# RWKV-7 inverse in a decoder step: three transfers of 68 and 34 rows, each split into two pieces

## The chip, the cores and the metric

The kernel runs on one core of a Trainium2 chip. The time is that of one execution on the device, in microseconds (us), from the launch of the program to its end; the median of three runs stands for a kernel. A profile is one further execution, recorded by the hardware profiler; its span runs from the first to the last instruction.

## The reference

One layer of a hybrid decoder is computed for 1024 prompt tokens and 8 samples of 8 tokens (1088 columns in all), with four token mixers side by side (HGRN2, RWKV-7, a convolution module, RG-LRU), then gates, output projection and an MLP. What matters here is the RWKV-7 mixer, which is a recurrence over tokens in each of 8 heads of width 64:

```
def step(s, inp):
    rt, wt, kt, vt, kkt, at = inp
    sa = jnp.einsum("bhvk,bhk->bhv", s, -kkt)
    s = s * wt[:, :, None, :] + sa[..., None] * (kkt * at)[:, :, None, :] + vt[..., None] * kt[:, :, None, :]
    return s, jnp.einsum("bhvk,bhk->bhv", s, rt)
```

All inputs and outputs are float32.

## The kernel before, in words

All matrices of the layer are multiplied on TensorE (PE) in blocks of 128 x 128, each product as three (high part by high part, low by high, high by low), into PSUM tiles named pg. The weights of a block are loaded by SP into wst, and ScalarE (ACT) and VectorE (DVE) form the high and low parts whi and wlo from them. The mixers run in four rounds (the string ROUNDS sets their order); each round has one RWKV block of two heads, one HGRN2 head pair, one convolution part and one RG-LRU part, and gate products fill PE in between. The generators of the mixers are written one after the other, and a scheduler with a cost model decides in which order the instructions stand on each engine. On an engine they then run strictly in that order.

An RWKV block (rw_block) does not walk through the tokens one by one. It takes chunks of 64 tokens, 16 of the prompt and one with the samples, so that with two heads there are 34 triangular systems of 64 x 64 to solve. For this, the unit triangular matrices are inverted. Each is cut into two diagonal blocks of 32 x 32 and one block beside them. The steps:

- PE computes the products G, DVE masks them into the tiles Gt (lines 554 to 565), and SP writes the diagonal blocks to DRAM, to za (line 569). za has the shape 2 x 34 x 32 x 32: half, unit, row, column.
- SP reads za back with one 32 x 32 block in each partition: 2 x 34 = 68 rows of 4 KB, tile At (line 585). Partition is now the unit, so that DVE can work on all 68 blocks at once.
- In 31 steps of two instructions each (lines 589 to 594), DVE forms the inverses in Zu.
- DVE copies the first 34 of them transposed into the place of At (line 596), SP writes Zu to DRAM as zb (68 rows of 4 KB, line 598) and the transposed copy as zx (34 rows of 4 KB, line 599).
- SP reads zx back into the tile X1 (line 602: 32 partitions with 34 pieces of 128 bytes each) and zb into the G tiles (lines 606 and 607: ten reads).
- PE multiplies: zq from X1 and the block beside the diagonal, ACT copies it into X1, zz from that copy and zb, ACT copies it into G (lines 608 to 620). Then the recurrence over the 17 chunks begins (line 631 on).

In between, the weights' reads stand in the same queue of SP: what is queued behind a read of zb that waits for its write stands still with it. The reads of zb stand for the writes of zb, that of X1 for the write of zx. The first matmuls that need X1 are zq; PE's queue holds pg products before and behind them. In PE's order the adaptive-norm weights (tile adaw, matmuls ada) come some 45 us behind zq in each round.

Of the kernel before, what the change touches and what calls it, by code (L numbers as in the profile page):

```python
# [90 lines left out]
class Net:  # L91
# [382 lines left out]
    def rw_block(self, j):  # L474
        nc = self.nc
# [22 lines left out]
        a, sg, wd = self.flat("a", 4), self.flat("sg", 5), self.flat("wd", 2)  # L498
# [52 lines left out]
        za = self.dp.tile([2, 34, 32, 32], F32, name="za", tag="za", bufs=2)  # L551
        zb = self.dp.tile([2, 34, 32, 32], F32, name="zb", tag="zb", bufs=2)
        zx = self.dp.tile([34, 32, 32], F32, name="zx", tag="zx", bufs=2)
# [28 lines left out]
        At = At_t[0:68, 0:1024].rearrange("p (i t) -> p i t", t=32)  # L582
        Zu_t = self.flat("Zu", 5)
        Zu = Zu_t[0:68, 0:1024].rearrange("p (i t) -> p i t", t=32)
        nc.sync.dma_start(At, za.rearrange("a u i t -> (a u) i t"))
        nc.gpsimd.memset(Zu_t[0:68, 0:1024], 0.0)
        nc.gpsimd.memset(Zu_t[0:68, 0:1024:33], 1.0)
        tm_t = self.rp.tile([128, 512], F32, name="tm", tag="vk", bufs=2)
        for i in range(31):
            r, m = i + 1, 31 - i  # L590
# [4 lines left out]
        xt_t = At_t  # L595
        nc.vector.tensor_copy(xt_t[0:34, 0:1024].rearrange("p (t i) -> p t i", i=32),
                              Zu[0:34].rearrange("p i t -> p t i"))
        nc.sync.dma_start(zb.rearrange("a u i t -> (a u) i t"), Zu)
        nc.sync.dma_start(zx, xt_t[0:34, 0:1024].rearrange("p (t i) -> p t i", i=32))

        X1 = self.flat("X1", 1)[:, 0:1088].rearrange("p (u t) -> p u t", t=32)
        nc.sync.dma_start(X1[64:96], zx.rearrange("u i t -> i u t"))
# [949 lines left out]
```

## Time and profile before

| | us |
|---|---|
| median of 3 runs | 2525.07 |
| lowest and highest | 2517.87, 2526.18 |
| profiled execution | 2528.64 |
| its span | 2526.9 |
| PE busy | 2430.2 (96%) |
| DVE busy | 1381.1 (55%) |
| ACT busy | 1037.1 (41%) |
| POOL busy | 330.2 (13%) |

The mean granted clock of TensorE over the span is 0.981 of full speed. The DMA engines move 300.46 MB in 185111 packets, 119 GB/s in the mean.

To read it: a row of a timeline has the start and the duration in us, the engine, the line, the operation, the written tile, an arrow and the read tiles, the shapes, the count, and in brackets the idle time of the engine before it with what ended it. The engine SPq is SP's queue of DMA issues; the duration of such a row is the issue, not the transfer. Buffer numbers are left out: X is X1, and At in a row of line 596 is the transposed copy. L98, L101, L104 and L107 are the lines of the helpers for ACT, DVE and PE, so that the tile says which instruction it is. In a list of waits stand the total in us, the number of times and the longest. In a table by stretches, a busy time is followed by the number of instructions in brackets; the granted clock (1.00 is full speed), the mean busy share of the 16 DMA engines and the GB/s end the row.

### The profile page before, as it was taken

What the parts mean: (1) busy time and instruction counts of PE and PEld (TensorE: products, weight loads), DVE (VectorE), ACT (ScalarE), POOL (GpSimd) and SP (SyncE); (2) the same over time, 40 slices, a digit from 0 to 9 for tenths busy, and PEclk for the clock granted to TensorE, in tenths of its full rate; (3) what the DMA queues carried; (4) which work ended last, traced back from release to release, by engine and by line L of the source; (5) the groups of instructions that cost most, each with busy time, mean ns of one, the idle gap of its engine ahead of it and who ended that gap; (6) DMA issues with size and microseconds to landing.
All of it is one profiled execution on the core that took longest, in us unless ns stands there. A gap on an engine that the chain in (4) does not pass through costs nothing.

```text
span 2526.9 us, 46611 instructions
## 1 busy us (share of the span) xinstructions
PE 2430.2 (96%) x19086; PEld 2255.0 (89%) x19086; DVE 1381.1 (55%) x2536; ACT 1037.1 (41%) x1855; POOL 330.2 (13%) x503
## 2 busy tenths in 40 slices
PE   6999999999999999999999999998899999999996
PEld 2897899898888988989888899998899999999996
DVE  6664626637365555457553667668755552422247
ACT  4512434323454235442244653346666665111115
POOL 3101210103100021101012000000222221000003
PEclk9999999999999999999999999999999999999998
DMA  6323132223221232112313455533565557434144
GB/s 242 120 85 91 56 104 68 70 74 98 92 68 63 81 97 97 68 62 80 98 60 105 163 186 169 194 114 104 157 157 157 157 153 257 137 139 184 61 158 132
DMA packets 185111, 300.46 MB, mean 119 GB/s; under 512 B 57385, under 2 KB 97273, under 8 KB 184897
## 3 DMA queue, kind: packets, MB, share of 16 engines
q1 hardware_dynamic: 134480, 217.79, 27.1%
q0 software_dynamic: 47104, 74.44, 9.7%
q10 hardware_dynamic: 3312, 5.25, 0.6%
q8 instruction: 150, 2.46, 0.4%
q14 instruction: 65, 0.52, 0.1%
HBM read 211.29 MB, written 81.66 MB: 116 GB/s over the span
## 4 chain that ended last, share of the span: by engine, by line
PE 79%; DVE 9%; DMA 6%; issue 3%; ACT 3%; SPq 0%; DVEq 0%; ACTq 0%; POOL 0%; POOLq 0%
PE pg L107 52%; PE pa L107 6%; PE pe L107 4%; PE sm L107 2%; PE pc L107 2%; PE pb L107 2%; PE ada L107 2%; PE pu L107 2%; DMA zx<-At 1%; DVE X L101 1%; DVE wlo L101 1%; PE G L107 1%; DMA adaw<-ada 1%; PE pyr L107 1%; PE po L107 1%
## 5 line engine op out<-in xcount | busy, mean ns | idle before, releaser
L107 PE MATMUL pg<-Hh,whi 128*128 128x362 f32 (+1 forms) x1872 | 631.5, 338 | 3.4 <-ACT Hh L98 3.1
L107 PE MATMUL pg<-Hh,wlo 128*128 128x362 f32 (+1 forms) x1872 | 632.6, 338 | 0.0
L107 PE MATMUL pg<-Hl,whi 128*128 128x362 f32 (+1 forms) x1872 | 625.2, 336 | 0.7 <-DVE Hl L104 0.6
L98 ACT ACTIVATE whi<-wst 128x512 fp32r<-128x512 f32 (+1 forms) x404 | 249.9, 620 | 617.0 <-PE pg L107 542.1
L101 DVE TENSOR_TENSOR wlo<-wst,whi 128x512 fp32r<-128x512 f32 (+1 forms) x404 | 280.3, 695 | 379.6 <-ACT whi L98 378.8
L107 PEld LDWEIGHTS pg<-Hh,whi 128*128 128x128 f32 x1872 | 357.4, 191 | 18.9 <-ACT Hh L98 5.9
L107 PEld LDWEIGHTS pg<-Hh,wlo 128*128 128x128 f32 x1872 | 357.8, 191 | 11.9 <-issue 4.2
L107 PEld LDWEIGHTS pg<-Hl,whi 128*128 128x128 f32 x1872 | 356.8, 191 | 10.1 <-issue 2.5
L107 PE MATMUL pg<-ah,whi 128*128 128x272 f32 x960 | 275.3, 289 | 4.3 <-ACT whi L98 4.3
L107 PE MATMUL pg<-ah,wlo 128*128 128x272 f32 x960 | 276.4, 290 | 0.6 <-DVE wlo L101 0.6
L107 PE MATMUL pg<-al,whi 128*128 128x272 f32 x960 | 273.0, 289 | 0.0
L107 PEld LDWEIGHTS pg<-ah,whi 128*128 128x128 f32 x960 | 180.9, 189 | 5.1 <-ACT whi L98 4.9
L107 PEld LDWEIGHTS pg<-ah,wlo 128*128 128x128 f32 x960 | 181.1, 189 | 1.6 <-DVE wlo L101 1.4
L107 PEld LDWEIGHTS pg<-al,whi 128*128 128x128 f32 x960 | 179.4, 189 | 0.0
L104 DVE SCALAR_TENSOR_TENSOR cacc<-u,pv,cacc 128x1024 f32<-128x1024 f32 x120 | 153.7, 1280 | 2.0
L104 DVE SCALAR_TENSOR_TENSOR R<-pg,mod,R 128x544 f32<-128x544 f32 (+2 forms) x120 | 65.7, 569 | 133.8 <-PE pg L107 133.8
L107 PE MATMUL pg<-yh,whi 128*128 128x362 f32 (+1 forms) x384 | 128.7, 335 | 0.9 <-DVE gt L101 0.9
L107 PE MATMUL pg<-yh,wlo 128*128 128x362 f32 (+1 forms) x384 | 127.5, 332 | 0.0
L107 PE MATMUL pg<-yl,whi 128*128 128x362 f32 (+1 forms) x384 | 127.1, 331 | 0.0
L1177 POOL DMA_DIRECT2D g<-gst x96 | 53.3, 555 | 399.0 <-ACT gst L98 383.5
L98 ACT ACTIVATE gst<-pg 128x362 f32<-128x362 f32 (+1 forms) x96 | 45.3, 472 | 134.8 <-PE pg L107 122.5
L689 POOL TENSOR_SCALAR sp<-St,dec 128x64 f32<-128x64 f32 x60 | 56.1, 935 | 231.0 <-DVE St L104 209.1
(446 smaller groups left out, 4819.3 us busy)
## 6 DMA issues: line engine op xcount, KB each, us to landing
wst<-w SPq DMA_DIRECT2D x136, 256.0 KB, 3.2
wst<-w_in SPq DMA_DIRECT2D x92, 256.0 KB, 2.8
gt<-g SPq DMA_DIRECT2D x32, 544.0 KB, 3.7
wst<-w_gate SPq DMA_DIRECT2D x64, 256.0 KB, 2.9
adaw<-ada SPq DMA_DIRECT2D x32, 512.0 KB, 5.3
ah<-ah POOLq DMA_DIRECT2D x60, 272.0 KB, 2.7
al<-al POOLq DMA_DIRECT2D x60, 272.0 KB, 4.3
ah<-ah SPq DMA_DIRECT2D x30, 544.0 KB, 10.0
```

The costliest lines, as they stand in the source:

```text
L98: return self.nc.scalar.activation(out, in_, func, bias=bias, scale=scale)
L101: return self.nc.vector.tensor_tensor(out, a, b, op=op)
L104: return self.nc.vector.scalar_tensor_tensor(out, a, s, b, op0=op0, op1=op1)
L107: return self.nc.tensor.matmul(out, lhsT, rhs, start=start, stop=stop, skip_group_check=True)
L689: nc.gpsimd.tensor_scalar(sp, St, dec[:, c:c + 1], None, op0=OP.mult)
L1177: nc.gpsimd.dma_start(d[:, n0:n0 + n], t[:, :n])
```

## The change

The reads and writes of 68 and 34 rows become two transfers each. The read of za into At is split into rows 0 to 63 and rows 64 to 67. The write of zb is split in the same way, that of zx into rows 0 to 31 and rows 32 and 33. In the code, the writes of zx now stand ahead of those of zb. The reads of zx and zb, the computation and all tiles stay as they are.

```
-        nc.sync.dma_start(At, za.rearrange("a u i t -> (a u) i t"))
+        rows = (slice(0, 64), slice(64, 68))
+        for r in rows:
+            nc.sync.dma_start(At[r], za.rearrange("a u i t -> (a u) i t")[r])
...
-        nc.sync.dma_start(zb.rearrange("a u i t -> (a u) i t"), Zu)
-        nc.sync.dma_start(zx, xt_t[0:34, 0:1024].rearrange("p (t i) -> p t i", i=32))
+        for r in (slice(0, 32), slice(32, 34)):
+            nc.sync.dma_start(zx[r], xt_t[r, 0:1024].rearrange("p (t i) -> p t i", i=32))
+        for r in rows:
+            nc.sync.dma_start(zb.rearrange("a u i t -> (a u) i t")[r], Zu[r])
```

The change adds four lines, so that the lines behind it have other numbers: line 585 becomes 587, 598 and 599 become 603 and 601, 602 becomes 606, 606 and 607 become 610 and 611. Per block, SP issues three transfers more, 12 in all. The order in which they stand is the scheduler's, and the scheduler also places some instructions of the other engines anew; the rows that the prediction speaks of, in the second block, are in the prediction. In blocks 2 to 4 the writes stand on SP as zb (64 rows), zb (4), zx (32), zx (2); in block 1 as zb (64), zx (32), zx (2), zb (4).

## The prediction

> **What bounds the kernel now.** I read the page first, then the list of waits on PE, then the timelines of PE, SP and DVE around the one wait that touches the change, then the table by stretches for the clock and the DMA engines.
>
> The page gives the span, the busy shares and the chain that ended last:
>
> ```profile
> span 2526.9 us, 46611 instructions
> ...
> PE 2430.2 (96%) x19086; PEld 2255.0 (89%) x19086; DVE 1381.1 (55%) x2536; ACT 1037.1 (41%) x1855; POOL 330.2 (13%) x503
> ...
> PE 79%; DVE 9%; DMA 6%; issue 3%; ACT 3%; SPq 0%; DVEq 0%; ACTq 0%; POOL 0%; POOLq 0%
> PE pg L107 52%; PE pa L107 6%; PE pe L107 4%; PE sm L107 2%; PE pc L107 2%; PE pb L107 2%; PE ada L107 2%; PE pu L107 2%; DMA zx<-At 1%; DVE X L101 1%; DVE wlo L101 1%; PE G L107 1%; DMA adaw<-ada 1%; PE pyr L107 1%; PE po L107 1%
> ```
>
> PE is the bound: busy 96%, so the whole kernel holds 96.7 us in which PE does nothing. One transfer of the change, the write of zx, stands on the chain by name, with 1%. The list of what PE waited for says where such a transfer is paid:
>
> ```profile
> PE zq L107 <- DMA X<-zx: 13.2, 4, 3.5
> ...
> PE pa L107 <- DVE T2l L101: 4.4, 2, 3.1
> ```
>
> Four times, once in each RWKV block, PE stands still for the read of zx, 13.2 us together. The timeline of PE shows the four places (start, duration, then the idle time before):
>
> ```profile
> 196.21 1.73 PE L107 MATMUL zq<-X,G 32*32 32x32 f32 x32 [3.46 <-DMA X<-zx]
> ...
> 535.07 1.91 PE L107 MATMUL zq<-X,G 32*32 32x32 f32 x32 [3.32 <-DMA X<-zx]
> ...
> 876.25 1.91 PE L107 MATMUL zq<-X,G 32*32 32x32 f32 x32 [3.18 <-DMA X<-zx]
> ...
> 1213.86 1.91 PE L107 MATMUL zq<-X,G 32*32 32x32 f32 x32 [3.27 <-DMA X<-zx]
> ```
>
> PE came to zq at 192.75, 531.75, 873.07 and 1210.59 us (start less idle). The stall isn't all that is lost. The table by stretches, for the 7 us behind each stall (us, busy times of PE, PEld, DVE, ACT and POOL, granted clock, DMA share, GB/s):
>
> ```profile
> 196.20:203.20 7.00, 6.99 (x50) 6.93 (x51) 1.42 (x4) 1.58 (x3) 0.00 (x0) 0.52 0.31 66
> 535.10:541.90 6.80, 6.80 (x50) 6.74 (x51) 0.69 (x1) 1.58 (x3) 0.00 (x0) 0.55 0.30 65
> 876.30:883.10 6.80, 6.80 (x50) 6.74 (x51) 0.69 (x1) 1.58 (x3) 0.00 (x0) 0.54 0.30 66
> 1213.90:1220.60 6.70, 6.70 (x48) 6.64 (x49) 0.69 (x1) 1.58 (x3) 0.00 (x0) 0.51 0.33 70
> ```
>
> The granted clock is about 0.5 there, and equal matmuls start 0.30 us apart where they started 0.17 us apart before the stall:
>
> ```profile
> 192.26 0.33 PE L107 MATMUL pg<-Hl,whi 128*128 128x362 f32 x1
> 192.42 0.32 PE L107 MATMUL pg<-Hh,whi 128*128 128x362 f32 x1
> ...
> 199.24 0.50 PE L107 MATMUL pg<-Hl,whi 128*128 128x362 f32 x1
> 199.54 0.51 PE L107 MATMUL pg<-Hh,whi 128*128 128x362 f32 x1
> ```
>
> So 27.3 us run at 0.167/0.303 = 55% of speed, and 45% of them, 12.3 us, are lost besides the 13.2.
>
> **Why the read of zx is late.** SP's own timeline in the second block, then the table for two stretches of it and one of the read that follows:
>
> ```profile
> 523.34 0.28 SPq L598 DMA_DIRECT2D zb<-Zu  x1
> 524.46 0.25 SPq L599 DMA_DIRECT2D zx<-At  x1
> 530.17 0.32 SPq L606 DMA_DIRECT2D G<-zb  x1
> 532.77 0.32 SPq L602 DMA_DIRECT2D X<-zx  x1
> 533.14 0.56 SPq L607 DMA_DIRECT2D G<-zb  x1
> 533.74 0.45 SPq L606 DMA_DIRECT2D G<-zb  x1
> ```
> ```profile
> 526.50:528.00 1.50, 1.50 (x11) 1.50 (x10) 1.09 (x5) 0.63 (x1) 0.00 (x0) 1.00 0.26 82
> 529.50:531.00 1.50, 1.50 (x11) 1.50 (x10) 0.00 (x0) 0.12 (x1) 0.00 (x0) 1.00 0.12 49
> ...
> 534.00:534.50 0.50, 0.00 (x0) 0.00 (x0) 0.00 (x0) 0.00 (x0) 0.00 (x0) 0.92 1.32 208
> ```
>
> The write zb takes 6.83 us until its first read can start (523.34 to 530.17), zx 8.31 us (524.46 to 532.77). The DMA share says why: 0.26 of 16 engines are 4 while the 68 rows move, 0.12 are 2 while the 34 rows do, one after the other; the read X<-zx into 32 partitions keeps all of them busy (1.32 by this count). 82 GB/s over 4 engines are 20.5 GB/s for each, so a row of 4 KB takes 0.2 us. The two engines that zx uses carry 17 rows of zb and 17 of zx: 34 x 0.2 = 6.8 us.
>
> **The change, part by part.** *The writes.* With 64, 4, 32 and 2 rows over 16, 4, 16 and 2 engines, the busiest engine carries 4 + 1 + 2 + 1 = 8 rows, 26 fewer: 5.2 us less. That 64 and 32 rows use all 16 is an estimate from that read into 32 partitions: no row here shows a write of 64. [...]
>
> The smaller write does not come first in the program that is built. zx needs the copy on DVE, and SP's order in the second block was and is this (zb, zx: the writes to DRAM; G, X: the reads back):
>
> ```order
> L598 DMA zb<-Zu 68x1024
> L599 DMA zx<-At 34x1024
> L606 DMA G_4371<-zb 32x8x32
> L602 DMA X_4748<-zx 32x34x32
> L607 DMA G_4371<-zb 32x8x32
> ```
>
> Now, in the same place on SP:
>
> ```order
> L603 DMA zb<-Zu 64x1024
> L603 DMA zb<-Zu 4x1024
> L601 DMA zx<-At 32x1024
> L601 DMA zx<-At 2x1024
> L610 DMA G_4374<-zb 32x8x32
> L611 DMA G_4374<-zb 32x8x32
> L606 DMA X_4754<-zx 32x34x32
> ```
>
> X's read stands behind two reads of zb instead of one; both can go out while zx lands. Blocks 3 and 4 read the same; in block 1 the 4 rows of zb come last and X stands behind one G, which waits for them. One issue costs about 0.5 us (533.74 less 533.14 is 0.60). PE's order changes too; in block 2 it was (pg: products of the big matrices, zq: the first product of the inverse):
>
> ```order
> L107 MATMUL pg<-Hh_117,whi 128x362
> L107 MATMUL zq<-X_4748,G_4371 32x32 x8
> L107 MATMUL zq<-X_4748,G_4372 32x32 x8
> L107 MATMUL pg<-Hh_117,wlo 128x362
> L107 MATMUL pg<-Hl_125,whi 128x362
> ```
>
> and is now
>
> ```order
> L107 MATMUL pg<-Hh_117,whi 128x362
> L107 MATMUL pg<-Hh_117,wlo 128x362
> L107 MATMUL pg<-Hl_125,whi 128x362
> L107 MATMUL pg<-Hh_118,whi 128x362
> L107 MATMUL zq<-X_4754,G_4374 32x32 x8
> L107 MATMUL zq<-X_4754,G_4375 32x32 x8
> ```
>
> Three matmuls of 0.167 us moved ahead of zq, so that PE comes to it 0.5 us later, in blocks 2 to 4.
>
> Block 2: X issues at 532.77 - 5.2 + 0.5 (the second piece's issue) = 528.1. Its read takes 2.3 us (532.77 to 535.07), so it is there at 530.4; PE comes at 531.75 + 0.5 = 532.25. Spare: 1.9 us. Blocks 3 and 4 have the same stall within 0.14 us. Block 1: two more issues, 1.0 us, no shift of zq: the stall of 3.46 less 5.2 plus 1.0 leaves 0.7 us to spare. All four stalls go, and with no idle PE the clock stays up: 13.2 + 12.3 = 25.5 us.
>
> Bounds for a piece's time, from rows of the list of DMA issues (KB, median us to landing):
>
> ```profile
> ah<-ah POOLq DMA_DIRECT2D x60, 272.0 KB, 2.7
> ...
> za<-G SPq DMA_DIRECT2D x32, 32.0 KB, 1.6
> ...
> za<-Gs SPq DMA_DIRECT2D x8, 8.0 KB, 2.5
> ```
>
> 1.6 us below, the 6.83 of zb above. Zx's last piece, issued at 524.96 in block 2, would be there at 526.6, 527.7 (by 2.7 us) or 531.8. I take 2.7: the same bytes in 128 rows. It agrees with the 528.1 worked out by bytes.
>
> [...] The rows: 6.7 to 7.0 us at about 0.5 behind each stall. [...]
>
> *What is late next.* Everything behind zq in a block hangs on PE: while it waited, ACT waited for zq itself (5.41 us), and DVE for ACT. So what follows moves up as a whole:
>
> ```profile
> 537.01 0.59 ACT L98 ACTIVATE X<-zq 32x512 f32<-32x512 f32 x1 [5.41 <-PE zq L107]
> ...
> 201.71 0.69 DVE L101 TENSOR_TENSOR wlo<-wst,whi 128x512 fp32r<-128x512 f32 x1 [6.60 <-ACT whi L98]
> ...
> 204.33 1.10 PE L107 MATMUL zz<-G,X 32*32 32x32 f32 x29
> ```
>
> zz needs reads of zb, which go out some 5 us earlier as well, about as much as PE gains. The next wait is for the ada weights:
>
> ```profile
> 236.80 0.55 SPq L350 DMA_DIRECT2D adaw<-ada  x1
> ...
> 244.09 1.78 PE L107 MATMUL ada<-adaw,cs 128*32 128x512 f32 x4 [0.90 <-DMA adaw<-ada]
> ...
> 582.10 1.05 PE L107 MATMUL ada<-adaw,cs 128*32 128x512 f32 x4 [0.30 <-DMA adaw<-ada]
> ```
>
> That load is issued between the matmuls of the earlier pieces, so it moves up too. A wait of 0.90 us there came with slow matmuls (1.78), one of 0.30 not (1.05): a flip either way is worth from the 0.73 us of that row to 3 us, if it lasts the 7 us of the rows above (7 x 0.45). It goes into the range.
>
> *The read At<-za* moves at the same share; DVE waits for it in each block:
>
> ```profile
> 152.00:153.50 1.50, 1.50 (x11) 1.50 (x10) 0.00 (x0) 0.63 (x2) 0.00 (x0) 1.00 0.25 96
> ```
> ```profile
> DVE tm L101 <- DMA At<-za: 19.8, 4, 8.1
> ```
>
> With 4 + 1 rows on an engine instead of 17 it comes 12 x 0.2 = 2.4 us sooner, less the second issue: about 2. Between it and zq lie 31 steps on DVE, and PE has its pg matmuls as cover; with zq no longer waiting it adds nothing: 0, or up to 2 us more to spare. *12 more issues* on SP, 0.5 us each, lie where SP waited (5.71 us between 524.46 and 530.17): 0; without that cover, 6 us. *Other moves*: DVE's order changes where the MLP's forms are made, and PE waits 4.4 us there for one of them (the row T2l above): plus or minus that.
>
> Sum: the profiled execution took 2528.64 us (span 2526.9 and 1.7 around it), 3.6 above the median of 2525.07. 2528.64 - 25.5 = 2503.1; on the median 2499.6, said as 2500.
>
> **Rivals.** *Too little* (0.08): pieces take nearer the 6.83 us. In blocks 2 to 4, zx is there at 531.8 and X at 534.1, 1.85 us behind PE; in block 1 the last piece is there 1.0 + 6.83 = 7.8 us behind zx instead of 8.3, and 3.0 us remain. Of 13.2 us, 8.6 stay. If the clock falls in half the blocks, 4.6 + 6 = 10.6 us are gained: 2514. For it: no 64-row write in the trace. Against: 272 KB in 2.7 us.
>
> *Nothing from splitting* (0.05): the bytes, not the engine count, set the time; 0.5 us in three blocks come from the shift, 2524. [...] The share of 0.26 and 0.12 speaks against it, since here the whole transfers leave most engines idle.
>
> *Slower* (0.03): each further write lands 2.6 us behind the one ahead, as zx did behind zb (530.17 to 532.77), whatever its size. X would issue at 523.34 + 6.83 + 3 x 2.6 = 537.97, 5.2 us later than before; four blocks 21, less 1.5 for the shift: 2544. It decides from (9.43 - 6.83) / 3 = 0.87 us per piece on. Against: reads of 32 KB are issued 0.5 us apart and fill the engines together (share 1.32).
>
> *Not what it says*: the small write isn't first, but with 8 rows on the busiest engine that is worth 4 rows at most, 0.8 us; it is in the forecast.
>
> **How the numbers follow.** Forecast 0.84, too little 0.08, nothing 0.05, slower 0.03. A measurement of this kernel can tell about 0.3%, 7.6 us, from no change. The forecast is beyond it, too little mostly (0.07 of 0.08): faster 0.91; nothing and the rest of too little: same 0.06; slower 0.03. The forecast's own spread is plus or minus 8 us (half of the 8.3 us that the three runs span, and 4 for order and ada waits): 2492 to 2508; up to 2514 it takes in the rival next to it.
>
> **What would show it.** Right: no PE idle before zq or under 0.5 us; granted clock 1.00 in the 7 us behind it; X<-zx issued some 5 us after zb instead of 9.4; DMA share well above 0.26 while the rows move; what stands behind the four blocks' zq earlier by 6.4, 12.8, 19 and 25 us. Wrong: zq still waiting over 1 us, a clock of 0.5 behind it, or as much idle time new before zz or ada.

## The result and the profile after

The changed kernel takes 2501.09 us (median of 4 runs, 2497.95 to 2501.93), the kernel before, run beside it, 2525.62 (4 runs, 2517.87 to 2526.42). The ratio is 0.9906, with a 95% interval of 0.9891 to 0.9922: 24.5 us less, where 25.5 were forecast. The profiled execution took 2501.3 us.

Its page, the lines that answer to those of before:

```profile
span 2499.5 us, 46627 instructions
...
PE 2419.5 (97%) x19086; PEld 2248.1 (90%) x19086; DVE 1383.3 (55%) x2536; ACT 1037.4 (42%) x1855; POOL 331.7 (13%) x503
...
PE 85%; DVE 6%; DMA 3%; ACT 2%; issue 2%; SPq 0%; DVEq 0%; ACTq 0%; POOL 0%; POOLq 0%
```

PE's share of the chain rises from 79% to 85%, and DMA's falls from 6% to 3%. PE is idle for 80.0 us instead of 96.7, and it is busy for 10.7 us less with the same 19086 matmuls: that second part comes from the clock (0.986 of full speed in the mean instead of 0.981). The list of what PE waited for has no zq any more; it begins

```profile
PE ada L107 <- DMA adaw<-ada: 16.5, 3, 15.5
PE rms L107 <- DVE accs L101: 13.1, 3, 8.2
PE lv L107 <- issue: 6.7, 4, 2.3
```

PE's timeline at the four zq (no bracket: no idle time ahead), then the table for the 7 us behind each:

```profile
191.96 1.19 PE L107 MATMUL zq<-X,G 32*32 32x32 f32 x32
...
523.15 1.19 PE L107 MATMUL zq<-X,G 32*32 32x32 f32 x32
...
855.32 1.19 PE L107 MATMUL zq<-X,G 32*32 32x32 f32 x32
...
1186.33 1.19 PE L107 MATMUL zq<-X,G 32*32 32x32 f32 x32
```
```profile
192.00:199.00 7.00, 7.00 (x120) 6.74 (x119) 5.13 (x18) 2.23 (x5) 0.00 (x0) 1.00 0.27 69
523.10:530.10 7.00, 7.00 (x116) 6.69 (x116) 0.69 (x1) 2.16 (x5) 0.00 (x0) 1.00 0.17 47
855.30:862.30 7.00, 7.00 (x117) 6.72 (x117) 0.69 (x1) 2.19 (x5) 0.00 (x0) 1.00 0.31 83
1186.30:1193.30 7.00, 7.00 (x117) 6.71 (x117) 0.69 (x1) 2.18 (x5) 0.00 (x0) 1.00 0.19 48
```

The same zq that took 1.73 and 1.91 us takes 1.19, at a granted clock of 1.00, and some 117 matmuls fit into 7 us instead of 50. SP's timeline in the second block, and the table while the writes run and after:

```profile
514.31 1.03 SPq L603 DMA_DIRECT2D zb<-Zu  x2
515.41 1.01 SPq L601 DMA_DIRECT2D zx<-At  x2
517.35 0.32 SPq L610 DMA_DIRECT2D G<-zb  x1
517.72 0.44 SPq L611 DMA_DIRECT2D G<-zb  x1
518.27 0.38 SPq L606 DMA_DIRECT2D X<-zx  x1
```
```profile
514.40:516.40 2.00, 2.00 (x14) 2.00 (x13) 1.89 (x5) 0.00 (x0) 0.00 (x0) 1.00 0.70 213
516.40:517.40 1.00, 1.00 (x8) 1.00 (x7) 0.89 (x4) 0.00 (x0) 0.00 (x0) 1.00 0.79 246
517.40:518.30 0.90, 0.90 (x8) 0.90 (x7) 0.79 (x4) 0.19 (x1) 0.00 (x0) 1.00 0.04 10
```

The DMA share is 0.70 to 0.79 while the rows move, at over 200 GB/s, where it was 0.26 and 0.12. X's read goes out 3.96 us behind the first issue of zb instead of 9.43. In blocks 1, 3 and 4 it is 3.91, 5.30 and 3.98 us; in block 3 an issue of 1.10 us for a read of zb stands ahead of it.

**Where the time went.** The program is cut at the first pg<-yh, the end of the mixers. In before that was at 1431.39 us, now at 1401.15. Both kernels, one after the other:

```profile
0.00:1431.40 1431.40, 1382.51 (x11231) 1219.12 (x11231) 783.42 (x1430) 584.14 (x1071) 206.33 (x324) 0.98 0.29 92
```
```profile
0.00:1401.10 1401.10, 1365.88 (x11230) 1205.11 (x11230) 784.78 (x1430) 584.03 (x1071) 207.38 (x324) 0.99 0.29 94
1401.10:2499.50 1098.40, 1053.61 (x7870) 1042.94 (x7857) 598.57 (x1107) 453.32 (x785) 124.34 (x179) 0.97 0.50 154
```

In the mixers 30.3 us are gained: 13.7 of idle time (48.9 to 35.2) and 16.6 of busy time. The rest of the program takes 1098.4 us instead of 1095.5: 2.9 us are lost again. Further profiles show which of this belongs to the change.

### The profile page after: what moved, and what is told of

Its sections match the earlier page's. It is cut to its first block, busy times and chain, and to the rows that moved or that the text cites. A ratio compares the mean times of both kernels' runs of the same rounds, so it can differ in the third digit from the quotient of the medians.

```text
span 2499.5 us, 46627 instructions
## 1 busy us (share of the span) xinstructions
PE 2419.5 (97%) x19086; PEld 2248.1 (90%) x19086; DVE 1383.3 (55%) x2536; ACT 1037.4 (42%) x1855; POOL 331.7 (13%) x503
## 3 DMA queue, kind: packets, MB, share of 16 engines
q1 hardware_dynamic: 134672, 217.79, 27.4%
## 4 chain that ended last, share of the span: by engine, by line
PE 85%; DVE 6%; DMA 3%; ACT 2%; issue 2%; SPq 0%; DVEq 0%; ACTq 0%; POOL 0%; POOLq 0%
PE pg L107 58%; PE pa L107 6%; PE pe L107 4%; PE sm L107 3%; PE pc L107 2%; PE pb L107 2%; PE ada L107 2%; PE pu L107 2%; PE G L107 1%; PE pyr L107 1%; PE po L107 1%; DVE X L101 1%; DMA adaw<-ada 1%; DMA wst<-w 1%; DVE wlo L101 1%
## 5 line engine op out<-in xcount | busy, mean ns | idle before, releaser
L107 PEld LDWEIGHTS pg<-Hh,whi 128*128 128x128 f32 x1872 | 354.2, 189 | 19.4 <-ACT Hh L98 6.0
L107 PEld LDWEIGHTS pg<-Hl,whi 128*128 128x128 f32 x1872 | 353.5, 189 | 10.1 <-issue 2.5
```

The source lines that it names most:

```text
L107: return self.nc.tensor.matmul(out, lhsT, rhs, start=start, stop=stop, skip_group_check=True)
```

## The experiments

The theory is the one of the prediction: the transfer of 68 rows uses 4 of 16 engines (DMA share 0.26 in before) and that of 34 rows 2 (0.12), so that zb and zx load 34 rows onto the two engines that they share; the stall before zq that follows costs its length and, on top, the clock behind it. The rivals: it is the number or the size of the pieces; it is the order, zx ahead of zb; it is the read of At; or the new order of PE's instructions. Each kernel starts from the kernel before, or from the changed one where that is said. All of them compute the whole layer.

### One part of the change at a time

**e3_at_only**: only the read of At is split.

```
-        nc.sync.dma_start(At, za.rearrange("a u i t -> (a u) i t"))
+        for r in (slice(0, 64), slice(64, 68)):
+            nc.sync.dma_start(At[r], za.rearrange("a u i t -> (a u) i t")[r])
```

> Only the read of za into At is split (64 and 4 rows); PE's order is that of the kernel before. Theory: DVE's wait for At falls by about 2 us per block, the stall before zq stays at 3.2 to 3.5 us with the clock at 0.5 behind it, and the time stays at 2525 within 4 us. Rival (the earlier start of DVE's 31 steps carries part of the gain): zb issues 2 us earlier against PE, the stall falls to 1.3 us, and the time to 2517 or below.

Measured: 2524.84 us (10 runs), ratio 0.9996 (0.9985 to 1.0007). The four stalls before zq are 3.51, 3.46, 3.20 and 3.28 us. What At's read gains is waited for again on DVE: from 480 us to zq of the second block its wait for At falls from 3.2 to 0.8 us, and that for whi rises from 1.8 to 4.0. The worth of 0 holds.

**e4_writes**: the reverse, both writes split as in the change, At whole. PE's order is that of the changed kernel.

> The writes of zb and zx are split as in the change, the read of At is whole; PE's order is that of the changed kernel. Theory: 8 rows on the busiest engine, no stall before zq, clock 1.00 behind it: the whole gain, 2501 within 4 us. Rival (the split of At carries part of it): 2503 to 2509.

Measured: 2502.23 us (4 runs, 2500.62 to 2504.2), ratio 0.9904 (0.9889 to 0.9919), no stall before zq. Within the spread, the writes are the whole effect.

**e1_zx_only** and **e2_zb_only**: only one of the two writes is split. In e1_zx_only PE's order is word for word that of before, so that a gain can't come from the new order.

```
+        for r in (slice(0, 32), slice(32, 34)):
+            nc.sync.dma_start(zx[r], xt_t[r, 0:1024].rearrange("p (t i) -> p t i", i=32))
         nc.sync.dma_start(zb.rearrange("a u i t -> (a u) i t"), Zu)
-        nc.sync.dma_start(zx, xt_t[0:34, 0:1024].rearrange("p (t i) -> p t i", i=32))
```

> Only the write of zx is split (32 and 2 rows), zb and At whole; the order of instructions on PE is that of the kernel before. Theory (rows on the busiest DMA engine at 0.2 us each): 17 + 2 + 1 = 20 rows instead of 34, 2.8 us less, 0.5 us for the second issue: X's read goes out 2.3 us earlier, right behind the first read of zb. The stall before zq falls from 3.3 to about 1.0 us in each block, 4 us in all instead of 13.2. If so short a stall leaves the clock up, 21 us are gained (2504); if the clock still falls, 9 us (2516). Rival (zb's write is what holds everything): nothing, 2525. Rival (only the write of zx counts): no stall, 2500.

> Only the write of zb is split (64 and 4 rows), zx and At whole. Theory: 4 + 1 + 17 = 22 rows on the busiest engine instead of 34, 2.4 us less, 0.5 us for the issue, and PE comes to zq 0.5 us later: the stall falls from 3.3 to about 0.9 us, 3.6 us in all; 2504 with the clock up, 2516 with the clock falling as before. Rival (only the write of zx counts): stall as before, 2525. Rival (zb's write is what holds everything): no stall, 2500.

Measured: e1_zx_only 2506.54 us (4 runs, 2499.15 to 2508.74), ratio 0.9917 (0.9893 to 0.9941); e2_zb_only 2503.9 us (4 runs, 2500.91 to 2505.81), ratio 0.991 (0.989 to 0.993). The stalls, from PE's timeline of e1_zx_only, are shorter than expected:

```profile
196.60 1.19 PE L107 MATMUL zq<-X,G 32*32 32x32 f32 x32 [0.70 <-DMA X<-zx]
...
1192.00 1.19 PE L107 MATMUL zq<-X,G 32*32 32x32 f32 x32 [1.21 <-DMA X<-zx]
```

In the two blocks between they are 0.73 and 0.58 us. In e2_zb_only only 0.56 and 0.40 us are left, in two blocks, where 3.6 in all were expected. By the counts of the expectations either write alone takes about half of the 26 rows off the busiest engine (34 to 20 with zx split, to 22 with zb split; some 2.5 us). In the second block X's read goes out 6.80 us (e1_zx_only) and 7.00 us (e2_zb_only) behind the first issue of zb instead of 9.43, and of a stall of 3.3 us little is left. It brings most of the gain, because the clock stays up behind stalls as short as these: in the 7 us behind the first three of e1_zx_only, 0.58 to 0.73 us long, the granted clock is 1.00, and behind the 1.21 us in block 4 it falls to 0.50 for 3.4 us. That e1_zx_only gains 19.4 us (against 2525.94 of the kernel before, run beside it) with PE's old order rules the new order out as the main cause.

### Is it the pieces, the order, or the engines?

**e5_halves**: zb in two pieces of 34 rows, as many as zx has, whose DMA share of 0.12 in before is 2 engines; PE's order is that of before.

```
-        nc.sync.dma_start(zb.rearrange("a u i t -> (a u) i t"), Zu)
+        for r in (slice(0, 34), slice(34, 68)):
+            nc.sync.dma_start(zb.rearrange("a u i t -> (a u) i t")[r], Zu[r])
```

> Only zb is split, but into 34 and 34 rows; PE's order is that of the kernel before. Theory: each half goes over 2 engines, so the busiest carries 17 + 17 + 17 = 51 rows instead of 34: X's read 3.4 us later and 0.5 for the issue, the stall 3.3 + 3.9 = 7.2 us per block, 29 us in all, DMA share 0.12 while all of them move; the clock loses what it lost before: 2541. Rival (splitting as such, more pieces in flight at once, is what helps): stall shorter than 3.3 us, 2525 or below.

Measured: 2532.57 us (10 runs), ratio 1.0017 (1.0000 to 1.0033), with stalls of 5.38, 4.98, 5.40 and 4.94 us. SP's timeline in the second block, and the table while the first half moves:

```profile
523.18 0.58 SPq L599 DMA_DIRECT2D zb<-Zu  x2
524.31 0.23 SPq L600 DMA_DIRECT2D zx<-At  x1
528.73 0.32 SPq L607 DMA_DIRECT2D G<-zb  x1
531.33 0.32 SPq L608 DMA_DIRECT2D G<-zb  x1
534.24 0.30 SPq L603 DMA_DIRECT2D X<-zx  x1
```
```profile
526.50:528.00 1.50, 1.50 (x11) 1.50 (x10) 1.13 (x4) 0.63 (x1) 0.00 (x0) 1.00 0.12 49
```

The sign is right: the DMA share of 0.12 is that of two engines, so that this split doesn't raise the number of engines, and the stalls are longer than the 3.18 to 3.46 us of before. The size was expected too large (2541 us, with a stall of 7.2 us): X's read goes out 11.06 us behind the first issue of zb, 1.6 us later than in before and not 3.9. Two things make the difference. 17 rows more on two engines come 2.6 and 2.9 us apart, 0.15 to 0.17 us a row, not 0.2. And the first half, with 17 rows on each engine, can be read after 5.55 us, where the whole zb, with 17 rows on each engine too, took 6.83; why was not traced.

**e8_pad**: no split of the writes at all; they are padded to 80 and 48 rows, of which the added ones are read by nobody. At's read is split. The lines shown are the writes; the DRAM tiles and the part of Zu that is set to zero grow with them.

```
-        nc.sync.dma_start(zb.rearrange("a u i t -> (a u) i t"), Zu)
-        nc.sync.dma_start(zx, xt_t[0:34, 0:1024].rearrange("p (t i) -> p t i", i=32))
+        nc.sync.dma_start(zx, xt_t[0:48, 0:1024].rearrange("p (t i) -> p t i", i=32))
+        nc.sync.dma_start(zb, Zu_t[0:80, 0:1024].rearrange("p (i t) -> p i t", t=32))
```

> The writes are not split but padded to multiples of 16: zb to 80 rows, zx to 48 rows (the rows added are never used), At split as in the change. Theory: 16 engines carry 5 + 3 = 8 rows, as many as the change's busiest, with one issue each: no stall before zq, 2501 within 4 us. Rival (the number of pieces, not of engines, matters): stall as before, 2525.

Measured: 2499.14 us (4 runs, 2498.41 to 2502.3), ratio 0.9894 (0.9879 to 0.9909), no stall before zq. More bytes in fewer transfers do as well as the split: it is neither the bytes nor the number of pieces.

**e9_zx23** and **e10_zx31**: the changed kernel with zx cut at other places. The orders of PE and DVE are those of the changed kernel.

```
-        for r in (slice(0, 32), slice(32, 34)):
+        for r in (slice(0, 23), slice(23, 34)):
```

> The changed kernel with zx cut into 23 and 11 rows instead of 32 and 2; the order of PE's and DVE's instructions is that of the changed kernel. [...] The busiest engine gets some 21 rows more than with 32 and 2; at 0.17 to 0.2 us a row X's read goes out 3.6 to 4.2 us later, and of the 2.5 us to spare before zq a stall of 1.1 to 1.7 us is left in each block. If stalls of that length keep the clock up (as 1.63 to 1.86 us did in e6_order): 4 to 7 us slower than the changed kernel, 2505 to 2508 us. If the clock falls behind them as behind 3.3 us: 12 us more, 2517 to 2520. Rival (bytes and number of pieces set the time): two pieces as before, no stall, 2501 us.

> The changed kernel with zx cut into 31 and 3 rows; the order of PE's and DVE's instructions is that of the changed kernel. Theory (engine count): 31 rows lie on one engine. The busiest engine gets some 28 rows more; at 0.17 to 0.2 us a row X's read goes out 4.8 to 5.6 us later than in the changed kernel and PE stands 2.3 to 3.1 us before zq in each block, 9 to 12 us in all. If the clock falls behind that as it did behind 3.2 to 3.5 us, another 12 us: 2522 to 2525, the whole gain is gone. If it doesn't fall: 2510 to 2513. Rival (bytes and number of pieces): 32 and 2 or 31 and 3 are the same, no stall, 2501 us.

Measured: e9_zx23 2516.97 us (7 runs), ratio 0.9972 (0.9958 to 0.9986); e10_zx31 2526.15 us (10 runs), ratio 1.0002 (0.9988 to 1.0016). Moving one row from the first piece to the second, 32 and 2 to 31 and 3, loses the whole gain. SP's timelines in the second block of e9_zx23, then of e10_zx31:

```profile
517.62 1.03 SPq L603 DMA_DIRECT2D zb<-Zu  x2
518.73 0.61 SPq L601 DMA_DIRECT2D zx<-At  x2
...
525.61 0.30 SPq L606 DMA_DIRECT2D X<-zx  x1
```
```profile
523.63 1.03 SPq L603 DMA_DIRECT2D zb<-Zu  x2
524.74 0.95 SPq L601 DMA_DIRECT2D zx<-At  x2
...
533.08 0.30 SPq L606 DMA_DIRECT2D X<-zx  x1
```

From zb to X's read it is 7.99 and 9.45 us against 3.96: 4.03 and 5.49 more, inside what was expected. From 23 to 31 rows the time from zx to X's read grows from 6.88 to 8.34 us, 0.18 us a row. In e9_zx23 the DMA share is 0.06 from 525.00 to 525.25 us, just ahead of X's read. The table of e10_zx31 while the 31 rows move has the same share, which is one engine of 16:

```profile
530.00:532.50 2.50, 2.50 (x16) 2.23 (x14) 0.00 (x0) 0.48 (x1) 0.00 (x0) 1.00 0.06 25
```

The packets that the traces record say the same. From 527.0 to 532.8 us of e10_zx31 one packet of 4 KB is under way at a time for 5.3 of the 5.8 us. In before it is two for 3.1 of the 4.2 us from 528.3 to 532.5, when two engines still have rows to write. In the changed kernel 16 and more are under way at once where it is most.

The stalls are 1.40 to 1.82 us in e9_zx23 (6.6 in all) and 2.99 to 3.78 in e10_zx31 (13.8), a little above the 1.1 to 1.7 and 2.3 to 3.1 that were expected. For e9_zx23, neither branch of the expectation was right about the clock, and its premise was a misreading of e6_order (below). The clock does fall, but for half as long. The table for the fall in the first block and around it, and for the falls in the three others:

```profile
193.80:195.10 1.30, 1.30 (x33) 1.26 (x34) 0.51 (x2) 0.07 (x1) 0.00 (x0) 1.00 0.43 66
195.10:198.51 3.41, 3.41 (x12) 3.41 (x13) 0.00 (x0) 1.43 (x3) 0.00 (x0) 0.50 0.50 116
198.52:199.52 1.00, 1.00 (x7) 1.00 (x7) 0.89 (x2) 0.07 (x1) 0.00 (x0) 1.00 0.01 1
529.62:533.02 3.40, 3.40 (x12) 3.40 (x12) 0.69 (x1) 1.50 (x3) 0.00 (x0) 0.50 0.27 53
864.12:867.53 3.41, 3.41 (x23) 3.35 (x20) 0.00 (x0) 1.51 (x3) 0.00 (x0) 0.50 0.43 108
1202.04:1205.45 3.41, 3.41 (x21) 3.35 (x19) 0.05 (x1) 1.58 (x3) 0.00 (x0) 0.50 0.46 108
```

With the 45% of the prediction, 6.6 of stall and 4 x 3.41 x 0.45 = 6.1 of clock are 12.7 us over the changed kernel's 2501.1, 2513.8. The interval of e9_zx23 is 2514 to 2521: the sum lies at its lower end, 0.7 us below the profiled run (2514.45) and 3.2 below the median. For e10_zx31, whose falls last 6.83 us, 13.8 + 12.3 = 26.1 give 2527.2; measured are 2526.15.

**e7_first**: the changed kernel with zx held ahead of zb on SP, so that the smaller write does come first.

```
-            nc.sync.dma_start(zx[r], xt_t[r, 0:1024].rearrange("p (t i) -> p t i", i=32))
+            zxw = nc.sync.dma_start(zx[r], xt_t[r, 0:1024].rearrange("p (t i) -> p t i", i=32))
         for r in rows:
-            nc.sync.dma_start(zb.rearrange("a u i t -> (a u) i t")[r], Zu[r])
+            zbw = nc.sync.dma_start(zb.rearrange("a u i t -> (a u) i t")[r], Zu[r])
+            self.after(zbw, zxw)
```

> The change with the write of zx really ahead of that of zb on SP, and X's read ahead of zb's. Theory: zq does not wait in the changed kernel, so nothing is left to gain: 2501 within 4 us, X's read issued about 2.5 us behind zx instead of 2.9. Rival (the order in the change's title is worth something of its own): 2497 or below.

Measured: 2499.17 us (4 runs, 2496.48 to 2501.07), ratio 0.9891 (0.9875 to 0.9907). This can't be told from the change: with both writes split, the order is worth nothing that shows.

**e6_order**: the kernel before, unsplit, with zx held ahead of zb in the same way.

> No split. The write of zx stands ahead of that of zb on SP in all blocks, and X's read ahead of zb's. Theory: zx's 17 rows go first on their 2 engines, 3.4 us, while zb waits: X's read goes out about 5.5 us behind zx's issue instead of 8.3, and the stall before zq falls from 3.3 to 0.5 us. zb then ends where zx ended before, so its reads go out 2 to 3 us later and zz becomes the next to wait, by up to 1 us. 2503 to 2510. Rival (order is worth nothing since both writes share the engines): stall as before, 2525.

Measured: 2537.41 us (10 runs, 2529.07 to 2548.05), ratio 1.0047 (1.0029 to 1.0066): slower, where 2503 to 2510 were expected. The mechanism that was tested worked (stalls before zq 1.86, 1.63, 1.86 and 1.18 us), but one held order made the scheduler place much of the program anew, and the time was lost elsewhere. One such place, in PE's timeline and in the table:

```profile
247.41 1.92 PE L107 MATMUL ada<-adaw,cs 128*32 128x512 f32 x4 [3.15 <-DMA adaw<-ada]
```
```profile
195.50:198.90 3.40, 3.40 (x13) 3.40 (x12) 0.00 (x0) 0.93 (x3) 0.00 (x0) 0.51 0.61 128
246.74:260.39 13.65, 12.61 (x55) 8.12 (x55) 5.43 (x6) 1.14 (x3) 1.66 (x3) 0.50 0.16 50
```

The ada weights come 3.15 us late (0.90 before), and the clock is at half for 13.65 us. That is about 6.4 (2.25 and 0.45 x 12.61, less the 1.5 that before lost to a fall there) of the 13.2 us by which zq of the second block comes later than before (548.25 us); the rest is not traced. So this run says nothing of what the order alone would be worth. Its first row corrects a reading too: zq itself still ran at full speed (1.19 us), and from that the expectation of e9_zx23 took it that the clock was kept. It fell 2 us later, for 3.4 us.

### A second execution, and both variants together

**e11_after_again** is the changed kernel, unaltered.

> The changed kernel once more, unaltered, for a second profile. Theory (the clock falls of the late part, at 1690 to 1757 us, 2110 to 2117 and 2468 to 2479 us, differ from execution to execution): no stall before zq, idle time of PE 80 us within 3, but the time lost to the clock differs from the 26.5 us of the first profile by over 2 us and the slow stretches of the late part lie at other places. Rival (they belong to the program): the same slow stretches at the same places, 26.5 us within 1.

Measured: 2497.96 us, one run. Its table, cut at the first pg<-yh:

```profile
0.00:1400.80 1400.80, 1364.03 (x11230) 1203.47 (x11230) 784.44 (x1430) 583.93 (x1071) 207.78 (x324) 1.00 0.29 94
1400.80:2496.10 1095.30, 1048.84 (x7867) 1038.28 (x7856) 597.95 (x1107) 453.02 (x785) 124.02 (x179) 0.98 0.50 155
```

The mixers take the same time within 0.4 us. The rest takes 1095.3 us instead of 1098.4, as long as in before (1095.5): PE is busy 4.8 us less with the same work. The busy time that is lost to the clock over the whole span (one less the granted clock, times the busy time, over stretches of 2 us) is 18.6 us instead of 26.5. The idle time is 83.2 us, just outside of the 80 within 3 that were expected. Not all falls of the late part move: those at 1690 us and from about 2465 us come in both executions, the one at 2110 us only in the first. Over all profiles of this document, with the writes split or not, the time behind the first pg<-yh lies between 1093.6 and 1098.9 us. So nothing shows that the 2.9 us that the first profile lost behind the mixers are the change's; they are within what differs from one execution to the next.

**e12_pad_first**: e8_pad with zx held ahead of zb.

> The writes padded to 80 and 48 rows and not split, and zx held ahead of zb on SP; the read of At split. If neither more pieces nor the order matters once all engines are used: as e7_first and e8_pad, 2499 us within 5, no stall before zq. If the two add up (each was 1.9 us below the changed kernel, within the noise): 2497. If the new order of the scheduler costs something, as in e6_order: over 2505 us, with the waits of PE elsewhere than at zq.

Measured: 2504.53 us (6 runs, 2498.21 to 2506.49), ratio 0.9912 (0.9897 to 0.9927). The two do not add up. There is no stall before zq, but in the last round waits of 0.97 us before ada and 0.70 us between ada's two steps have the clock at 0.55 in the mean from 1230 to 1245 us, some 6 us. No version tried is better than the change by more than the measurement can tell.

## Why the prediction was right, step by step

- **The four stalls, 13.2 us.** All four are gone; the idle time up to the end of the mixers falls by 13.7. Right.
- **The clock, 12.3 us.** The four falls behind zq, 6.83 us each, are gone. Right as a term, but the busy time of the mixers falls by 16.6. The profile of before has slow stretches that answer to none of the changed kernel, at 244 us behind the ada wait (3.4 us) and at 746 us (6.8 us). In e3_at_only, with PE's order and the stalls of before, both are missing too, and the first pg<-yh comes at 1426.87 us instead of 1431.39; so the 4.3 us over the forecast are most likely chance of the one profile. Measured against e3_at_only, the mixers gain 25.7 us. The prediction took the length of the fall from its rows, 6.7 to 7.0 us, and the runs show 3.4 us behind stalls of 1.18 to 1.86 us and 6.8 behind those of 2.99 to 3.78. For this kernel's stalls, 3.18 to 3.46 us, the rows were the right measure.
- **The busiest engine, 34 rows to 8, 5.2 us.** X's read goes out 5.5 us sooner behind zb where 4.7 net were worked out (5.2 less one issue), and the spare time in the second block is 523.15 less 518.27 and some 2.4 for the read, 2.5 us instead of 1.9. In blocks 1, 3 and 4 it is 2.0, 1.1 and 2.5 us, where 0.7, 1.9 and 1.9 were forecast. Of the engine counts behind it, the DMA shares show 4 for 68 rows (0.26 in before), 2 for 34 (0.12 in before and in e5_halves) and one for 31 (0.06 in e10_zx31). That 64 and 32 rows go over 16 was an estimate; in the changed kernel the share is 0.70 to 0.79 and 16 packets of 4 KB and more are under way at once. That 4 rows go over 4 engines and 2 over 2, as the 8 rows of the sum have it, no run shows; what the runs showed in its place is the 5.5 us of X's read. The price of 0.2 us a row is too high: the second row of the prediction's own table, 49 GB/s over two engines, gives 0.17, the experiments give 0.15 to 0.18, and a packet of 4 KB takes 0.159 us in the median of the trace of before. At that price 26 rows are 4.1 us, 3.6 net. So 1.9 of the 5.5 us are not covered by the count of the rows, and where they come from is open; that 4.7 came so near is in part luck. The 21 rows more on the busiest engine in the expectation of e9_zx23 were the author's estimate: of its two pieces no run shows on how many engines the 11 rows lie, and for the 23 there is the one share of 0.06. Measured in their place are the 4.03 us by which X's read goes out later than in the changed kernel, and the 0.18 us for each row from 23 to 31.
- **At's split, 0.** Right (e3_at_only). In the changed kernel DVE waits 10.1 us for At's reads instead of 19.8, but between zb's issue and PE's coming to zq the time in the second block is 8.8 us against 8.4, which is the shift by three matmuls.
- **12 more issues, 0.** Right: SP's issues stand where it waited before.
- **The smaller write is not first, and that is worth at most 0.8 us.** Not contradicted: e7_first is 1.9 us faster, which is within the spread, so that 0.8 us can't be told from 0.
- **Block 1's ada wait.** The wait of 0.90 us became 0.65, and the fall of 3.4 us that before has behind it is gone. This is the flip that the range allowed for.
- **What stands behind the four zq, 6.4, 12.8, 19 and 25 us earlier.** The last zq of each block (zq<-X,Gs) come 7.2, 14.6, 23.6 and 30.3 us earlier. But in e3_at_only, where the stalls stayed, those of blocks 3 and 4 are 5.1 and 5.0 us earlier too, so that some 25 us of the last figure are the change's.
- **The sum, 25.5.** Between the spans of the profiled executions it is 27.4 for the first profile of the changed kernel and 30.8 for the second, between the medians 24.5. Executions of the same program differ by 3.4 us between these two profiles and by 8.6 us among the four runs of before, so an agreement within 1 us is more than the single terms, of which some were off, could promise.
- **Rivals.** Too little: no stall stayed. Nothing from splitting: e8_pad and e10_zx31 speak against bytes and pieces. Slower, each further write 2.6 us later: that happens in e5_halves (2.6 and 2.9 us), where the pieces don't use more engines, not here.

## What to carry to other kernels

Count the rows of a transfer before its bytes: here 68 and 34 rows of 4 KB kept 4 and 2 of the 16 DMA engines busy (shares 0.26 and 0.12), and in the second block X's read went out 9.43 us behind the first issue of zb. With the writes cut at 64 and 32 rows it went out after 3.96 us, with them padded to 80 and 48 rows after 4.33, and no stall was left; with zx cut at 31 it took 9.45 us and nothing was gained. Price a stall of PE with the clock behind it: here each stall of 1.18 us or more before zq had the clock at half for 3.4 to 10.2 us behind it, which by the 45% of the prediction is an estimated 1.5 us lost for each 3.4. Read the granted clock for some 10 us behind a stall, not only at the next instruction. Where a scheduler decides the order, look first at what an edit moves: e6_order shortened the stall that it aimed at and was slower.

## What the runs showed of the hardware that was not expected

**The clock fell and rose on a grid of 3.413 us.** In the rows of e9_zx23 above, the falls begin at 195.10, 529.62, 864.12 and 1202.04 us and last 3.40 to 3.41 us; the distances of 334.52, 334.50 and 337.92 us are 98.0, 98.0 and 99.0 times 3.413 us, and each fall lasts one such step. The falls of before lie on a grid of the same step too; its table for the first and the microsecond behind it, and the three others:

```profile
196.50:203.33 6.83, 6.83 (x47) 6.77 (x44) 1.51 (x5) 1.58 (x3) 0.00 (x0) 0.50 0.31 67
203.33:204.33 1.00, 1.00 (x8) 0.78 (x6) 0.89 (x4) 0.00 (x0) 0.00 (x0) 1.00 0.61 219
534.42:541.25 6.83, 6.18 (x46) 6.12 (x47) 0.50 (x1) 1.58 (x3) 0.00 (x0) 0.50 0.37 76
875.75:882.58 6.83, 6.33 (x47) 6.27 (x48) 0.65 (x1) 1.58 (x3) 0.00 (x0) 0.50 0.34 72
1213.67:1220.50 6.83, 6.64 (x48) 6.58 (x49) 0.69 (x1) 1.58 (x3) 0.00 (x0) 0.50 0.35 72
```

The distances are 99, 100 and 99 steps, and 6.83 us are two. How long the clock stayed low went by the stall before zq:

| stall before zq | seen in | clock at 0.5 |
|---|---|---|
| 0.40 to 0.73 us | e1_zx_only (3 blocks), e2_zb_only (2) | not at all |
| 1.18 to 1.86 us | e1_zx_only (block 4), e6_order (4), e9_zx23 (4) | 3.4 us |
| 2.99 to 3.78 us | before (4), e3_at_only (4), e10_zx31 (4) | 6.8 us |
| 4.94 to 5.40 us | e5_halves (4) | 6.8 us (2), 10.2 us (2) |

Stalls of 1.2 us ahead of zq were enough for a fall (1.18 us in e6_order, 1.21 in e1_zx_only), and in before 0.90 us ahead of ada (a fall of 3.4 us at 244.29 us). The length alone does not decide: in e5_halves stalls of 5.38 and 4.98 us brought 6.8 us and stalls of 5.40 and 4.94 brought 10.2. What separates one step from two, the length or its place on the grid, no run shows.

**PE was busy and the clock fell all the same.** In the changed kernel PE has no idle time from 419.5 to 427.23 us, and yet the clock is at half from 423.82 us on for one step; the timeline shows what runs ahead of it:

```profile
420.95 1.95 PE L107 MATMUL po<-hq,sst 128*128 128x8 f32 x16
```
```profile
419.50:423.82 4.32, 4.32 (x32) 4.02 (x31) 0.88 (x1) 0.85 (x2) 0.16 (x2) 1.00 0.00 0
423.82:427.23 3.41, 3.41 (x14) 3.41 (x13) 2.32 (x4) 1.12 (x2) 0.54 (x1) 0.50 0.11 44
```

Sixteen matmuls of 8 columns take 1.95 us of the step before the fall. In the second execution the clock falls there too, in before at 432 us. These sixteen matmuls come once in each round, so that the fourteen profiles have 56 such places, with the grid at offsets that differ: a step begins at 423.82 us in the changed kernel and at 424.27 us in its second execution. The clock falls at all 22 places where a step of the grid begins 1.87 to 3.00 us behind the start of the sixteen, and at none of the 34 others, where a step begins up to 1.78 us or from 3.35 us behind it. So these falls belong to this stretch of the program, and whether one came went by the place of the grid at all 56. Whether the matmuls of 8 columns are the reason, or the other small ones next to them as well, was not tried by itself. The two executions of the changed kernel differ in the offset, and in other falls too: at 2110 to 2117 us the clock was at 0.51 in the first profile of the changed kernel, and at 1.00 there in the second. PE's busy time, 2419.49 against 2412.86 us for the same instructions, goes with the 26.5 and 18.6 us that the clock takes in them.
